# A hybrid encoder step on one core: attention's steps are taken up 0.8 later by the planner's clock

## The chip, the cores and the metric

One core of a Trainium2 chip runs the whole step as one program. The time is device microseconds of an execution; of the kernel before there are three, and the median counts. A further execution was profiled. The engines are TensorE (PE, with its weight loads as PEld), VectorE (DVE), ScalarE (ACT), GpSimd (POOL) and SyncE (SP), which starts most DMAs.

## The reference: what is computed

Two groups of rows (1024 of a prompt, 64 of a sample) go through one layer. Cut to what matters here:

```python
h = rms_norm(x, n_pre)
aq, af, ai, ag, bq, bk, bv, bg, cu, cg = split(h @ w_in)      # 1024 x 3584
# stick-breaking attention, 4 heads of 64, blocks of 128 queries
z = einsum('bqhd,bkhd->bhqk', q, k) * 64 ** -0.5
log_1m = where(mask, log_sigmoid(-z), 0)
after = cumsum(log_1m, reverse=True) - log_1m
w = where(mask, exp(log_sigmoid(z) + after), 0)
b_out = einsum('bhqk,bkhd->bqhd', w, v) * silu(bg)
x = x + rms_norm(concat([a_out, b_out, c_out]) @ w_out, n_post)
x = x + rms_norm(cross_attn(rms_norm(x, nx_pre), mem_k, mem_v), nx_post)
```

Beside attention stand an HGRN2 scan (a_out), a pooling mix (c_out) and the keys and values of 256 memory rows. All outputs are float32.

## The kernel before

**Tiling.** The 1088 rows are nine row tiles (i = 0 to 7 of 128 prompt rows, i = 8 of 64 sample rows), and three column chunks c = 0, 1, 2 of 384, 384 and 320 rows where activations lie transposed. Large products keep precision by splitting both operands into a high and a low half and adding three products (`mm3`, line 339): "main products" below are these, with tile name mm in the trace. `mm3` hands control back after every six products, so main work comes in groups of six; a projection of one chunk (`proj`, line 713) is 24 products, four groups.

**The order is planned.** The kernel is written as generators, and a planner (`Sched`, lines 43 to 100) decides in which order they are run on. Every helper (`mm`, `tr`, `act`, `tt` and so on) adds a cost for its instruction to a clock for its engine (`op`, line 56), and each task remembers when its last results on each engine are due (`dep`). A task's ready time is the latest of these due times, TensorE's left out, or the time at which what it waits for by name was done, plus the task's `slack` (`ready`, line 71). Main is the last task in the list. The planner runs the first task whose ready time has passed on its TensorE clock, so any other task that is ready goes ahead of main, and main's groups fill the time between. A task that gives control back is looked at again at the next such point. A product of 384 columns and high and low halves costs max(0.113, 384 / 2400 + 0.005) us by that clock (line 170).

The planner's order is the order in which instructions are written down, and with it their priority. The program builder then places them with a reckoning of its own: where a buffer is not free by that reckoning, a later instruction can go first. Instructions under `urgent()` (evacuations of main products, splits of weights) are given a higher priority.

**The stage around the change.** After the HGRN2 heads, main projects bq, bk and bv of head pair 0, then of pair 1 (`keys_values`, line 947); each chunk of bv spawns a small task, `bv{j}{c}`, that transposes the values to rows. While pair 1 is projected, w_out is loaded and split in three pieces (`load_wide`, line 1011; tiles wraw, hhi, hlo). Main then goes over the row tiles: `side` (line 1193) splits a row tile of the mixed heads (C), `wide` (line 1203) multiplies it by w_out in pieces of 384, 384 and 256 columns (four groups each), and `wide_norm` normalizes and adds the residual. Row tile i waits for `("sb", 0, i)` and `("sb", 1, i)`, which attention marks as done.

Attention is one task, `sb` (`sb_all`, line 614), spawned with the first chunk's values of pair 0. Its 26 units (13 to a pair) are a row tile's queries against up to 512 keys; row tiles 4 to 7 take two units. A step of the task is `scores` of unit k, `values` of unit k - 2 and `weights_T` of unit k - 1, then it gives control back:

- `scores` (line 629): three products and a mask for each of the two heads of the pair, on the upper and the lower 64 rows, into two banks of the PSUM tiles hg (three in all); for each head two sigmoids on ScalarE, a scan (line 650) and a product on VectorE, tile sm.
- `weights_T` (line 658): up to eight transposes (tp) and two copies on ScalarE (wT).
- `values` (line 677): up to sixteen products (hg from wT and vb); at a row tile's last unit VectorE multiplies the bank into C.

Pair 1's units wait for `bv10`, `bv11` and `bv12` where they begin to need them (line 703). When `sb` is finished, the next row tile to end closes attention's buffers and opens those of the next norm (`open_h2`, line 1172), whose task `h2` runs with a slack of 2.0.

Of the kernel before, what the change touches and what calls it, by code (L numbers as in the profile page):

```python
# [104 lines left out]
def hybrid_step(  # L105
# [38 lines left out]
    sch = Sched()  # L144
# [5 lines left out]
    def ps_tp():  # L150
        return ps.tile([P, 512], F32, tag="tp", name="tp", bufs=2)
# [21 lines left out]
    def tr(out, in_, n):  # L173
        sch.op("PE", 0.11)
        PE.transpose(out, in_, ident[:n, :n])  # L175

    def act(out, in_, func, **kw):
        t = TABLE.get(func)
        sw = 1.3 if t is not None and t != cur.get("table") else 0.0
        if t is not None:  # L180
            cur["table"] = t
        sch.op("ACT", 0.2 + sw + free(in_) / 1200.0)
        cur['ACT'] = ACT.activation(out, in_, func, **kw)  # L183
# [20 lines left out]
    def urgent():  # L204
        return tc.high_priority(offset=URGENT)
# [83 lines left out]
    def split(src, hi, lo):  # L289
        act(hi, src, AF.Copy)  # L290
        sub(lo, src, hi.bitcast(F32))
# [421 lines left out]
    def proj(wb, c, hT, every=6):  # L713
        t0, n = CHUNKS[c]
        o = ps_mm()
        hhi, hlo = hT[c]
        yield from mm3(o[:, :n], [(wb[0][:, k], wb[1][:, k], hhi[:, k, :n], hlo[:, k, :n]) for k in range(KT)], every)
        cur["o"] = o
# [14 lines left out]
    def main():  # L733
# [4 lines left out]
        pool = TP("start", "right")  # L738
# [9 lines left out]
        def prefetch(i):  # L748
            if i < len(names):
                kind, j = names[i]  # L750
                src = w_xk[j] if kind == "mk" else w_xv[j] if kind == "mv" else w_in[COL[kind] // P + j]
                if i < 2:
                    wq[i] = [wpool([P, KT, P], F32, "wraw", 2), wpool([P, KT, P], F32R, "whi", 2),
                             wpool([P, KT, P], F32R, "wlo", 2), {}]
                    first.append(wq[i])
                    for ks in (slice(0, 4), slice(4, 8)):
                        SP.dma_start(wq[i][0][:, ks], src[:, ks])
                else:
                    wq[i] = wblock(src)
# [184 lines left out]
        st, sbops = {}, {}  # L944
        wo, wdeps = [], []

        def keys_values(bi, j, wbs, q):


            kh = pool([P, KEYS], F32R, "kh", 2)  # L950
            kl = pool([P, KEYS], F32R, "kl", 2)
            ck = pool([P, P], F32, "ck", 1)
            SP.dma_start(ck, cache_sb_k[j * P:(j + 1) * P, :])
            split(ck, kh[:, SEQ:SEQ + P], kl[:, SEQ:SEQ + P])
            vb = pool([P, NT, P], F32, "vb", 2)
            cv = pool([P, P], F32, "cv", 2)
            SP.dma_start(cv, cache_sb_v[0, 0, :, 2 * j:2 * j + 2, :])
            sbops[j] = (q, (kh, kl), vb, cv)
            rows, cs = slice(j * P, (j + 1) * P), slice(j * P, (j + 1) * P)
            for c, (t0, n) in enumerate(CHUNKS):  # L960
                n1 = min(n, SEQ - t0)
                sch.fresh(**wbs[0][2])
                yield None
                yield from proj(wbs[0], c, hT)
                o = cur["o"]
                kr = pool([P, 384], F32, "kr", 3)
                with urgent():
                    split(o[:, :n1], kh[:, t0:t0 + n1], kl[:, t0:t0 + n1])
                    if n1 < n:
                        split(o[:, n1:n], kh[:, SEQ + P:], kl[:, SEQ + P:])  # L970
                    act(kr[:, :n], o[:, :n], AF.Copy)
                SP.dma_start(p_sb_k[rows, t0:t0 + n1], kr[:, :n1])
                if n1 < n:
                    SP.dma_start(s_sb_k[rows, :], kr[:, n1:n])
                sch.fresh(**wbs[1][2])
                yield None
                yield from proj(wbs[1], c, hT)
                o = cur["o"]
                vr = pool([P, 384], F32, "kr", 3)
                with urgent():  # L980
                    act(vr[:, :n], o[:, :n], AF.Copy)

                def values_tm(vr, c, t0, n, n1):
                    yield None
                    if c:
                        yield f"bv{j}{c - 1}"
                    pt = ps_tp().rearrange("p (c t) -> p c t", t=P)
                    i0, full = t0 // P, n1 // P
                    for i in range(full):
                        tr(pt[:, i, :], vr[:, i * P:(i + 1) * P], P)  # L990
                    if n1 < n:
                        tr(pt[:SMP, full, :], vr[:, n1:n], P)
                    act(vb[:, i0:i0 + full, :], pt[:, :full, :], AF.Copy)
                    SP.dma_start(p_sb_v[0, 0].rearrange("(i p) h d -> p i (h d)", p=P)[:, i0:i0 + full, cs],
                                 vb[:, i0:i0 + full, :])
                    if n1 < n:
                        act(vb[:SMP, 8, :], pt[:SMP, full, :], AF.Copy)
                        SP.dma_start(s_sb_v[0, 0].rearrange("p h d -> p (h d)")[:, cs], vb[0:SMP, 8, :])
                sch.spawn(values_tm(vr, c, t0, n, n1), f"bv{j}{c}")
                if (j, c) == (0, 0):  # L1000
                    sch.spawn(sb_all(sbops, pool), "sb")
                if j == 1:
                    b0, b1 = PIECES[c]
                    pair = [big([P, KT, n], F32R, f"{x}{c}") for x in ("hhi", "hlo")]
                    wdeps.append(load_wide(w_out, pair, range(b0, b1)))
                    wo.append((slice(b0 * P, b1 * P), *pair))
                elif c == 1:
                    prefetch(bi + 2)
                    prefetch(bi + 3)

        def load_wide(src, tiles, blocks):
            save, sch.cur = sch.cur, Sched.Task(None, "w")
            hi, lo = tiles
            for i, cb in enumerate(blocks):
                with urgent():
                    raw = wload(src[cb])
                    cs = slice(i * P, (i + 1) * P)
                    act(hi[:, :, cs], raw, AF.Copy)
                    sub(lo[:, :, cs], raw, hi[:, :, cs].bitcast(F32))
            dep, sch.cur = dict(sch.cur.dep), save  # L1020
            return dep
        for bi, (kind, j) in enumerate(names):
# [16 lines left out]
            if (kind, j) in (("bk", 0), ("bk", 1)):  # L1039
                wbs = [wq.pop(bi), wq.pop(bi + 1)]  # L1040
                yield from keys_values(bi, j, wbs, st["bq"])
# [17 lines left out]
            if kind in ("mk", "mv"):  # L1059
# [30 lines left out]
                if (kind, j) == ("mv", KT - 1):  # L1090
# [4 lines left out]
                    pool = TP("hgrn", "right")  # L1095
# [65 lines left out]
            elif kind == "bg" and j == 1:  # L1161
# [4 lines left out]
                pool = TP("sb", "right")  # L1166
# [293 lines left out]
```

## Time and profile before

| | us |
|---|---|
| three executions, median | 937.71 |
| lowest, highest | 934.66, 938.21 |
| profiled execution, its own time | 935.02 |
| its span | 933.3 |
| attention of pair 0, from its first scores | 441.6 to 494 |
| main products alone | 494 to 516.8 |
| attention of pair 1 | 516.8 to 576 |

The mean granted TensorE clock of the profiled execution is 0.996 of full speed. In the rows of the profile a line starts with the source line (L171 is the product helper, L175 the transpose, L183 ScalarE's, L187 VectorE's two-operand helper), then engine and operation, then output tile and input tiles with shapes, a count and times. In rows of a timeline the start comes first, then the length; a bracket at the end is the engine's idle time before it and what ended it. In rows of windows every engine has its busy time and, in brackets, its count of instructions, then come the granted clock, the DMA share and GB/s. Lengths of products include a modelled end and overlap, so that the starts tell the pace. PE's busy time counts overlaps once.

### The profile page before, as it was taken

What the parts mean: (1) busy time and instruction counts of PE and PEld (TensorE: products, weight loads), DVE (VectorE), ACT (ScalarE), POOL (GpSimd) and SP (SyncE); (2) the same over time, 40 slices, a digit from 0 to 9 for tenths busy, and PEclk for the clock granted to TensorE, in tenths of its full rate; (3) what the DMA queues carried; (4) which work ended last, traced back from release to release, by engine and by line L of the source; (5) the groups of instructions that cost most, each with busy time, mean ns of one, the idle gap of its engine ahead of it and who ended that gap; (6) DMA issues with size and microseconds to landing.
All of it is one profiled execution on the core that took longest, in us unless ns stands there. A gap on an engine that the chain in (4) does not pass through costs nothing.

```text
span 933.3 us, 18372 instructions
## 1 busy us (share of the span) xinstructions
PE 914.2 (98%) x7504; PEld 853.6 (91%) x7504; DVE 556.6 (60%) x1125; ACT 479.5 (51%) x1005; POOL 107.2 (11%) x194
## 2 busy tenths in 40 slices
PE   8899999999999999999999999999999999999997
PEld 7899999999998999989779788999999999999997
DVE  6849483674678574552684777565564545563343
ACT  7623384658767774963673765433452333342231
POOL 5502430010010010000000000211200000001110
PEclk9999999999999999999999999999999999999999
DMA  8815511011100111012111411222433111232231
GB/s 306 259 38 181 142 46 47 25 49 29 47 27 31 47 33 46 25 47 79 47 31 36 157 61 69 90 68 80 164 119 92 30 39 46 76 106 91 91 101 58
DMA packets 33126, 73.60 MB, mean 79 GB/s; under 512 B 5601, under 2 KB 18065, under 8 KB 33042
## 3 DMA queue, kind: packets, MB, share of 16 engines
q1 hardware_dynamic: 30112, 68.07, 22.7%
q0 software_dynamic: 1888, 4.35, 1.3%
q8 instruction: 59, 0.97, 0.4%
q14 instruction: 25, 0.20, 0.1%
q10 hardware_dynamic: 1042, 0.01, 0.1%
HBM read 56.45 MB, written 15.89 MB: 78 GB/s over the span
## 4 chain that ended last, share of the span: by engine, by line
PE 82%; DVE 6%; ACT 4%; DMA 4%; issue 2%; POOL 1%; DVEq 0%; POOLq 0%; ACTq 0%
PE mm L171 64%; PE hg L171 14%; PE tp L175 5%; DVE sm L650 3%; DVE sm L187 1%; DVE wlo L187 1%; ACT L183 1%; ACT whi L183 1%; DMA xt<-in_x_prompt_dram 1%; DVE hlo L187 1%; DMA wraw<-in_w_xk_dram 1%; DMA mkd<-mraw 1%; DMA wraw<-in_w_xo_dram 1%; DMA gT<-in_norm_mem_dram 1%; DMA mvd<-mtm 1%
## 5 line engine op out<-in xcount | busy, mean ns | idle before, releaser
L171 PE MATMUL mm<-hhi,whi 128*128 128x384 f32 (+2 forms) x1272 | 425.1, 334 | 0.0
L171 PE MATMUL mm<-hlo,whi 128*128 128x384 f32 (+2 forms) x1272 | 412.5, 325 | 0.0
L171 PE MATMUL mm<-hhi,wlo 128*128 128x384 f32 (+2 forms) x1248 | 405.3, 325 | 0.0
L171 PEld LDWEIGHTS mm<-hhi,whi 128*128 128x128 f32 x1272 | 239.2, 188 | 6.3 <-issue 1.3
L171 PEld LDWEIGHTS mm<-hlo,whi 128*128 128x128 f32 x1272 | 239.5, 188 | 1.2 <-issue 0.9
L171 PEld LDWEIGHTS mm<-hhi,wlo 128*128 128x128 f32 x1248 | 234.6, 188 | 0.4 <-issue 0.3
L187 DVE TENSOR_TENSOR wlo<-wraw,whi 128x1024 fp32r<-128x1024 f32 (+1 forms) x53 | 63.5, 1200 | 56.6 <-ACT whi L183 56.3
L183 ACT ACT_TABLE_LOAD x66 | 84.7, 1283 | 19.0 <-DVE E L187 12.0
L183 ACT ACTIVATE whi<-wraw 128x1024 fp32r<-128x1024 f32 (+1 forms) x53 | 55.3, 1043 | 71.5 <-PE mm L171 54.7
L183 ACT ACTIVATE wraw<-mm 128x384 f32<-128x384 f32 (+3 forms) x51 | 22.9, 449 | 72.8 <-PE mm L171 62.9
L650 DVE TENSOR_TENSOR_SCAN sm<-sm 128x384 f32<-128x384 f32 (+4 forms) x52 | 48.3, 938 | 14.0 <-ACT sm L183 14.0
L183 ACT ACTIVATE sm<-hg 128x384 f32<-128x384 f32 (+4 forms) x104 | 42.2, 485 | 15.7 <-PE hg L171 8.7
L187 DVE TENSOR_TENSOR wraw<-mm,gain 128x384 f32<-128x384 f32 (+1 forms) x48 | 24.4, 510 | 41.6 <-ACT wraw L183 41.3
L1241 POOL TENSOR_TENSOR small<-small 128x1 f32<-128x1 f32 (+1 forms) x18 | 4.2, 234 | 375.3 <-ACT wraw L183 375.3
L183 ACT ACTIVATE E<-E 128x512 f32<-128x512 f32 (+1 forms) x68 | 32.8, 515 | 10.5 <-DVE E L187 9.9
L171 PE MATMUL mm<-mhi,wlo 128*128 128x256 f32 x128 | 35.8, 289 | 1.8 <-DVE wlo L187 1.8
L321 POOL TENSOR_TENSOR small<-small,mhalf 128x1 f32<-128x1 f32 (+2 forms) x50 | 36.0, 719 | 4.2
L171 PE MATMUL mm<-mhi,whi 128*128 128x256 f32 x128 | 36.2, 293 | 0.1
L171 PE MATMUL mm<-mlo,whi 128*128 128x256 f32 x128 | 35.1, 283 | 0.0
L443 POOL COPY qf<-q 128x512 f32<-128x512 f32 (+1 forms) x12 | 14.6, 1218 | 177.6 <-PE hg L171 140.7
L187 DVE TENSOR_TENSOR wlo<-C,whi 128x1024 fp32r<-128x1024 f32 x16 | 19.6, 1225 | 24.9 <-ACT whi L183 23.4
L191 DVE SCALAR_TENSOR_TENSOR C<-wraw,small,C 128x384 f32<-128x384 f32 (+3 forms) x54 | 27.8, 569 | 10.2 <-POOL small L321 10.2
(209 smaller groups left out, 1409.1 us busy)
## 6 DMA issues: line engine op xcount, KB each, us to landing
wraw<-in_w_in_dram SPq DMA_DIRECT2D x28, 512.0 KB, 3.6
xt<-in_x_prompt_dram SPq DMA_DIRECT2D x8, 512.0 KB, 6.5
wraw<-in_w_xv_dram SPq DMA_DIRECT2D x8, 512.0 KB, 3.9
wraw<-in_w_out_dram SPq DMA_DIRECT2D x8, 512.0 KB, 3.6
C<-in_x_prompt_dram SPq DMA_DIRECT2D x8, 512.0 KB, 3.5
x1d<-C SPq DMA_DIRECT2D x8, 512.0 KB, 2.8
wraw<-in_w_xq_dram SPq DMA_DIRECT2D x8, 512.0 KB, 3.6
wraw<-in_w_xo_dram SPq DMA_DIRECT2D x8, 512.0 KB, 3.6
```

Of the source, the lines that this page charges most:

```text
L171: cur['PE'] = PE.matmul(out, lhsT=lhsT, rhs=rhs, start=start, stop=stop, skip_group_check=True)
L175: PE.transpose(out, in_, ident[:n, :n])
L183: cur['ACT'] = ACT.activation(out, in_, func, **kw)
L187: cur['DVE'] = DVE.tensor_tensor(out=out, in0=a, in1=b, op=op)
L191: DVE.scalar_tensor_tensor(out=out, in0=a, scalar=s, in1=b, op0=op0, op1=op1)
L321: POOL.tensor_tensor(out=r[:n, :w], in0=r[:n, :w], in1=mhalf[:n, :w], op=ALU.pow)
L443: POOL.tensor_copy(qf[:, 1, :], qq)
L650: DVE.tensor_tensor_scan(m[:nq, :n][:, ::-1], m[:nq, :n][:, ::-1], m[:nq, :n][:, ::-1], 1.0 if p is None else p[:nq, 0:1], ALU.mult, ALU.min)
L1241: POOL.tensor_tensor(out=ms[:n, 0:1], in0=ms[:n, 0:1], in1=ms[:n, pi:pi + 1], op=ALU.add)
```

## The change

The attention task is spawned with a slack of 0.8 where it had none. The slack is added to its ready time at every look that the planner takes at it, so it holds for each of its steps and for its waits by name.

```diff
@@ -998,7 +998,7 @@
                 sch.spawn(values_tm(vr, c, t0, n, n1), f"bv{j}{c}")
                 if (j, c) == (0, 0):
-                    sch.spawn(sb_all(sbops, pool), "sb")
+                    sch.spawn(sb_all(sbops, pool), "sb", 0.8)
                 if j == 1:
```

The code that reads it, unchanged:

```python
    def ready(self, t):
        if t.wait is not None:
            if t.wait not in self.done:
                return None
            return max([self.done[t.wait]] + [v for e, v in t.dep.items() if e != "PE"]) + t.slack
        return max([0.0] + [v for e, v in t.dep.items() if e != "PE"]) + t.slack
```

## The prediction

> **What bounds the kernel now.** I read the page's engine shares first, then the busy time of each engine by stage, then who makes TensorE wait in the attention's stage, and last the single steps in the timeline.
>
> ```profile
> span 933.3 us, 18372 instructions
> PE 914.2 (98%) x7504; PEld 853.6 (91%) x7504; DVE 556.6 (60%) x1125; ACT 479.5 (51%) x1005; POOL 107.2 (11%) x194
> ```
>
> TensorE is the bound. All its recorded idle time is 933.3 - 914.2 = 19.1 us, and only what lies where attention runs is within reach of an edit that respaces attention. Attention runs in two bursts, one for each pair of heads. The stages, with all engines (the columns after the length are busy time and count of PE, PEld, DVE, ACT, POOL):
>
> ```profile
> 441.50:494.00 52.50, 49.97 (x418) 40.01 (x418) 40.86 (x72) 36.27 (x89) 0.00 (x0) 1.00 0.13 39
> 494.00:516.80 22.80, 22.80 (x137) 22.53 (x135) 6.50 (x10) 8.43 (x14) 0.00 (x0) 1.00 0.26 84
> 516.80:576.10 59.30, 58.00 (x485) 45.22 (x484) 48.51 (x82) 42.26 (x105) 0.20 (x1) 1.00 0.21 68
> ```
>
> The same stretches, main products alone (tile mm):
>
> ```profile
> 441.50:494.00 52.50, 22.07 (x116) 18.50 (x116) 1.73 (x4) 3.41 (x8) 1.00 0.13 39
> 494.00:516.80 22.80, 22.72 (x132) 22.19 (x132) 2.16 (x4) 3.36 (x7) 1.00 0.26 84
> 516.80:576.10 59.30, 23.61 (x127) 19.44 (x126) 1.72 (x4) 3.15 (x9) 1.00 0.21 68
> ```
>
> Three things are in these rows. TensorE idles 52.50 - 49.97 = 2.53 us in the first burst and 59.30 - 58.00 = 1.30 us in the second, 3.83 us together. Between the bursts 132 main products, 22 groups of six, run with no attention beside them, in 22.72 us: 1.03 us a group. And the granted clock is 1.00 throughout, so no idle time is paid for twice. VectorE is busy for 78% and 82% of the two bursts: close enough to full that a single long instruction in its queue is felt. What TensorE waits for inside the bursts:
>
> ```profile
> PE tp L175 <- DVE sm L187: 2.3, 3, 1.3
> PE hg L171 <- DVE C L187: 0.9, 1, 0.9
> PE hg L171 <- ACT wT L183: 0.5, 2, 0.3
> ```
>
> That is 3.7 of the 3.83 us: the transposes wait for the weights from VectorE, value products wait for a PSUM bank that VectorE has not read out, and for weights that ScalarE has not copied. All of them are operands that are late at a step taken up too soon. The worst one, on PE and then on DVE:
>
> ```profile
> 458.52 0.31 PE L171 MATMUL mm<-hlo,whi 128*128 128x320 f32 x1
> 458.66 0.31 PE L171 MATMUL mm<-hhi,wlo 128*128 128x320 f32 x1
> 458.90 0.46 PE L171 MATMUL hg<-kh,qh 64*128 64x384 f32 x2
> ...
> 459.65 0.28 PE L171 MATMUL hg<-negmask,identb 128*128 128x128 bf16 x2
> 461.23 1.12 PE L175 MATMUL tp<-ident,sm 128*128 128x128 f32 x7 [1.30 <-DVE sm L187]
> ```
>
> ```profile
> 456.57 1.22 DVE L187 TENSOR_TENSOR wlo<-wraw,whi 128x1024 fp32r<-128x1024 f32 x1 [3.18 <-ACT whi L183]
> 457.71 0.42 DVE L187 TENSOR_TENSOR kl<-mm,kh 128x256 fp32r<-128x256 f32 x1
> 458.05 2.33 DVE L650 TENSOR_TENSOR_SCAN sm<-sm 128x512 f32<-128x512 f32 x2
> ...
> 460.41 1.28 DVE L187 TENSOR_TENSOR sm<-sm 128x511 f32<-128x511 f32 x2
> ```
>
> A weight's low half (1.22 us) and a key's (0.42 us) stand ahead of the scans, so the transposes start 1.30 us late.
>
> **The change, part by part.** Instructions are neither added nor removed; only the place of the attention's steps among the main products changes. The planner takes a step at the first boundary between groups of main products at which its TensorE clock has passed the step's ready time, so the overshoot now lies between nothing and one group. By the planner's own costs (line 170) a group of six is 6 x (384/2400 + 0.005) = 0.99 us, 0.83 us with 320 columns, 0.67 us with 256. With 0.8 added to the ready time, nearly every step goes one group later (with 384 columns when the overshoot is under 0.8 of 0.99; with 256 sometimes two). What an attention step issues is TensorE's products, ScalarE's sigmoids and copies and VectorE's scans and products; it starts no DMA, so no queue of SP or POOL is passed by it. The main products that come ahead of it bring their evacuations and the loads of w_out with them, and these start earlier against attention.
>
> Is there enough main work? The first burst has 13 steps before its units are scored, and needs 13 more groups; the 22 alone behind it give them, at no cost. In the second burst 127 products are 21 groups among 15 steps, and 9 of those groups now run alone, while attention waits for the last value block of its pair:
>
> ```profile
> 544.91 4.04 PE mm L171 x26
> ...
> 549.43 4.86 PE mm L171 x28
> ```
>
> With two groups to a step, main reaches that block after about five steps instead of eight, so this wait goes, and 30 groups in 15 steps reach some way into the second row tile of the output projection (9 groups of projections, then 12 to a row tile). Main does not run dry: its first row tile needs attention's first row tile of the second pair, which is read out two steps after it is scored, and comes up after nine groups, some four steps in. What is late next is the end of attention, by some 9 groups, 9 us, less what is saved. Behind it stands only the opening of the next norm's buffers, at the end of a row tile, so it may come one row tile (12 groups, 12.4 us) later. The cover for that:
>
> ```profile
> 588.69 1.05 ACT L183 ACTIVATE wraw<-C 128x1024 f32<-128x1024 f32 x1
> ```
>
> ```profile
> 600.00:610.00 10.00, 10.00 (x66) 9.97 (x64) 6.99 (x11) 4.11 (x11) 2.44 (x5) 1.00 0.31 107
> ```
>
> ```profile
> 667.96 13.53 PE mm L171 x78
> ```
>
> The norm's first tile starts at 588.69 and its first reader is the query projection at 667.96: 79 us for work that is caught up with VectorE at 70% and ScalarE at 41%, while TensorE stands at 10.00 of 10.00. I cost it at nothing; were the cover gone, the price would be one late tile, about the 1.3 us of such a stall.
>
> Now the gains. First, the idle 3.83 us. Second, waits that the modelled ends hide: sixteen value products take 1.58 us in the two short steps (64 queries) and 1.09 us elsewhere, so 0.49 us each, 0.98 us.
>
> ```profile
> 483.93 1.09 PE L171 MATMUL hg<-wT,vb 128*64 128x128 f32 x16
> 491.53 1.58 PE L171 MATMUL hg<-wT,vb 128*64 128x128 f32 x16 [0.27 <-ACT wT L183]
> 569.98 1.58 PE L171 MATMUL hg<-wT,vb 128*64 128x128 f32 x16 [0.26 <-ACT wT L183]
> ```
>
> Third, score pairs that have come apart. The two heads' scores run as pairs on the two halves of the rows; in three steps of the second burst the builder has placed one head at a time, because a bank is not yet free by its reckoning (ScalarE is splitting w_out there):
>
> ```profile
> 448.59 0.44 PE L171 MATMUL hg<-kh,qh 64*128 64x384 f32 x2
> 449.53 0.44 PE L171 MATMUL hg<-wT,vb 128*64 128x128 f32 x4
> 522.13 0.44 PE L171 MATMUL hg<-kh,qh 64*128 64x384 f32 x1
> 522.88 0.39 PE L171 MATMUL mm<-hhi,wlo 128*128 128x320 f32 x1
> 523.94 0.44 PE L171 MATMUL hg<-kh,qh 64*128 64x384 f32 x1
> 524.72 0.50 PE L175 MATMUL tp<-ident,kr 128*128 128x128 f32 x3
> 526.15 0.50 PE L171 MATMUL hg<-kh,qh 64*128 64x512 f32 x1
> 526.58 0.65 PE L175 MATMUL tp<-ident,sm 128*128 128x128 f32 x4
> 530.29 0.44 PE L171 MATMUL hg<-kh,qh 64*128 64x384 f32 x1
> 531.67 0.45 PE L171 MATMUL hg<-kh,qh 64*128 64x384 f32 x1
> ```
>
> A whole pair takes 449.53 - 448.59 = 0.94 us; apart, 0.75 + 0.78 = 1.53 us. The second visit also costs its two crossings: the start after 458.66 comes 0.24 us later instead of 0.14, so 0.1 on the way in and, as I estimate, as much out. A broken step costs 0.59 + 0.18 = 0.77 us; two are wholly broken and the one at 526.15 loses the 0.43 us of its lone product, 1.97 us in all. One more group gives ScalarE 1 us to free the banks.
>
> The sum: 3.83 + 0.98 + 1.97 = 6.8 us is what spacing could give. Of it stays: of the 1.30 us stall what a 320 column group (6 x 0.147 = 0.88 us) leaves, 0.4 us; another step that now meets a 1.22 us split, 0.3 us; one of the three broken steps, 0.7 us; and two extra visits where a new group parts steps that lie back to back, 0.4 us. 6.8 - 1.8 = 5.0 us. The profiled execution took 935.02 us (1.7 us beside its span), so 930.0 for one like it; it lies 2.7 us under the median of the runs shown, 937.71 (934.66 to 938.21), and on that median the forecast is 932.7 us. The bounds: all of it and more, or less than nothing if the steps come apart (below).
>
> The idle rows may not show all the room. In a step that nothing delays, the weight loads fill this much:
>
> ```profile
> 486.83:489.39 2.56, 2.56 (x28) 1.97 (x27) 2.46 (x4) 2.04 (x5) 0.00 (x0) 1.00 0.00 0
> ```
>
> 1.97 of 2.56 us is 77%. In the first burst 116 main products at 22.72 / 132 = 0.172 us take 20.0 us, all of it filled with loads, and attention's other 32.5 us at 77% would hold 25.0 us: 45.0 us of loads, where the row has 40.01. The second, 127 products or 21.8 us and 37.5 us at 77%, would hold 50.7, where the row has 45.22. That is 5.0 + 5.5 = 10.5 us short, at most, since some products are narrower than those of the 0.172 us; my sum above has 6.8. The Trainium skill, "Perfetto Trace Analysis", Identifying the Most-Contended Engine, says that matmul busy time misjudges TensorE's room because matmuls are pipelined, and that the loads' busy share is the better measure; by it the gain would be the larger one, and the trace of before cannot yet tell.
>
> **The rivals.** *More room than the idle rows show.* 10.5 - 1.8 = 8.7 us, 929.0 on the median. For it: the shortfall of loads just worked out. Against it: broken pairs and crossings lower the share of loads too, and are in my sum already.
>
> *The stalls only move.* The late operands come from 1.22 us splits that stand ahead in VectorE's queue; each still meets some step, and the builder places by its own reckoning, so that its order hardly follows the planner's. Then 0 to 2 us, 936 to 938. For it: VectorE's work is the same. Against it: with 13 more groups the first burst's VectorE share falls from 78% to 62%.
>
> *Slower: steps come apart.* The builder may fill the extra room by placing one head's scores at a time, as at 522 and 530. It decides from the point where the broken steps outweigh the rest of the gain: without the pairs that is 3.83 + 0.98 - 0.7 - 0.4 = 3.7 us, eaten by 5 steps of 0.77 us; 11 make the kernel slower by 4.7 us, and 12 of the 23 whole ones give 12 x 0.77 - 3.7 = +5.5 us, 943.2. For it: main's w_out splits now fall on fewer steps, and a crossing costs a tenth. Against it: the first burst has all 13 steps whole. The Trainium skill, "TensorEngine Tiling (Array Packing)", Key Properties, says that a change of tiling mode drains TensorE; the 0.24 against 0.14 us agrees, and by that rule every extra visit speaks against this edit.
>
> **How the numbers follow.** 0.5% of this kernel, 4.7 us, is about what a measurement of it can tell from no change. My forecast (2.5 to 7 us saved): 0.55, of which 0.30 over 4.7 us. More room: 0.12. Stalls move: 0.21. Steps come apart: 0.12. So faster by over 0.5%: 0.42; within: 0.25 + 0.21 = 0.46; slower: 0.12. The likeliest case's own range is 930.5 to 935. The range for 8 in 10 runs from 928.5 (the larger gain) to 939 (no gain, at the upper end of the runs), leaving out the broken steps and the far end of the gain.
>
> **What would show it.** Right: two groups, 12 main products, between most attention steps; the stretch without attention between the bursts falls from 22 groups to about 9, and that at 545 goes; PE idle in the bursts under 1.5 us; scores in pairs throughout; attention ends near 579. Wrong: one group as before (the edit did not reach the order); the idle rows still name DVE sm with over 2 us; more than 5 steps with single scores; or idle time after 580 that was not there.

## The result and the profile after

The changed kernel takes 929.28 us (median of five, 928.38 to 932.13), the kernel before 935.48 us (median of five, 934.02 to 938.21): a ratio of 0.994 with a 95% interval of 0.9923 to 0.9957, 6.2 us faster. Beside the last experiments it was timed again, 930.24 against 934.55 us, a ratio of 0.9955 (0.9939 to 0.997), 4.3 us. The forecast was 5.0 us less; as a time, 932.7 us, counted from the median of three, 937.71 us, that was known then.

The page of its profiled execution (930.88 us):

```profile
span 929.2 us, 18368 instructions
PE 911.1 (98%) x7504; PEld 853.1 (92%) x7504; DVE 556.8 (60%) x1125; ACT 479.6 (52%) x1005; POOL 107.7 (12%) x194
```

The number of instructions on each engine is as before. The bursts and what lies between them, all engines, then main products alone:

```profile
443.70:499.80 56.10, 55.02 (x454) 45.74 (x454) 42.69 (x72) 37.48 (x91) 0.00 (x0) 1.00 0.12 34
499.80:516.90 17.10, 17.10 (x100) 16.84 (x98) 6.22 (x10) 6.49 (x11) 0.00 (x0) 1.00 0.38 122
516.90:581.00 64.10, 63.01 (x533) 51.92 (x532) 51.48 (x88) 44.00 (x110) 1.86 (x4) 1.00 0.24 76
```

```profile
443.70:499.80 56.10, 27.84 (x152) 24.22 (x152) 2.68 (x6) 4.41 (x10) 1.00 0.12 34
499.80:516.90 17.10, 17.02 (x96) 16.49 (x95) 1.21 (x3) 2.46 (x5) 1.00 0.38 122
516.90:581.00 64.10, 31.36 (x175) 27.10 (x174) 3.17 (x7) 4.81 (x15) 1.00 0.24 76
```

Both bursts are longer and hold more main products, 152 for 116 and 175 for 127, and the stretch without attention is shorter, 96 products for 132. In the timeline 12 main products, two groups, lie between most steps where 6 or fewer lay before; the 54 products that ran alone near 545 are spread over the second burst.

The start of the kernel scatters from execution to execution (attention's first key transposes come at 441.25 us in this profile of the changed kernel and at 439.31 us in another), so I compare a stretch that holds the same work in every run: from the key transposes ahead of attention's first scores to the first product of row tile 8 (1605 products on TensorE). Before, and after:

```profile
440.11:660.44 220.33, 216.37 (x1606) 192.67 (x1605) 141.23 (x232) 119.11 (x283) 17.55 (x36) 1.00 0.21 71
```

```profile
441.25:656.39 215.14, 212.97 (x1605) 191.66 (x1604) 141.60 (x232) 119.00 (x283) 17.60 (x36) 1.00 0.22 73
```

The stretch is 5.2 us shorter; what follows it takes 272.8 and 272.9 us (929.2 - 656.4 and 933.3 - 660.4). Of the 5.2 us, idle time gives 3.96 - 2.17 = 1.8 us and TensorE's busy time 3.4 us. Busy time can shrink with the same products because it holds what the idle column doesn't show: waits inside merged rows, and pairs of scores that run one after the other. Both are gone in the short steps (1.09 us for 1.58) and at the three places where the pairs had come apart, two of which are shown:

```profile
497.69 1.09 PE L171 MATMUL hg<-wT,vb 128*64 128x128 f32 x16
...
524.81 0.45 PE L171 MATMUL hg<-kh,qh 64*128 64x384 f32 x2
...
529.67 0.51 PE L171 MATMUL hg<-kh,qh 64*128 64x512 f32 x2
...
573.04 1.09 PE L171 MATMUL hg<-wT,vb 128*64 128x128 f32 x16
```

What TensorE still waits for in the bursts:

```profile
PE tp L175 <- DVE sm L187: 1.1, 2, 0.8
PE hg L171 <- ACT sm L183: 1.1, 1, 1.1
```

Of the three kinds of late operands two are gone; the wait for weights from VectorE is halved, and one of 1.1 us is new: value products that wait for a bank which ScalarE's sigmoids have not yet read out.

```profile
466.54 1.09 PE L171 MATMUL hg<-wT,vb 128*64 128x128 f32 x16 [1.08 <-ACT sm L183]
```

### The profile page after: what moved, and what is told of

It reads as the page before. It is cut to its first block, busy times and chain, and to the rows that moved or that the text cites. A ratio compares the mean times of both kernels' runs of the same rounds, so it can differ in the third digit from the quotient of the medians.

```text
span 929.2 us, 18368 instructions
## 1 busy us (share of the span) xinstructions
PE 911.1 (98%) x7504; PEld 853.1 (92%) x7504; DVE 556.8 (60%) x1125; ACT 479.6 (52%) x1005; POOL 107.7 (12%) x194
## 4 chain that ended last, share of the span: by engine, by line
PE 87%; DVE 4%; ACT 3%; DMA 3%; issue 1%; POOL 1%; DVEq 0%; POOLq 0%; ACTq 0%
PE mm L171 66%; PE hg L171 16%; PE tp L175 5%; DVE sm L650 1%; ACT L183 1%; DVE hlo L187 1%; DVE wlo L187 1%; DMA wraw<-in_w_xk_dram 1%; DMA gT<-in_norm_mem_dram 1%; DMA xt<-in_x_prompt_dram 1%; DMA mkd<-mraw 1%; DMA wraw<-in_w_xv_dram 0%; ACT whi L183 0%; DMA wraw<-in_w_out_dram 0%; POOL small L321 0%
## 5 line engine op out<-in xcount | busy, mean ns | idle before, releaser
L183 ACT ACTIVATE E<-E 128x512 f32<-128x512 f32 (+1 forms) x68 | 32.8, 515 | 10.5 <-DVE E L187 9.8
L183 ACT ACTIVATE hhi<-tp 128x512 fp32r<-128x512 f32 (+1 forms) x36 | 19.1, 570 | 28.7 <-PE tp L175 28.6
```

## The experiments

Each was timed in turn with the kernel before on one chip. The stretch is the one of equal work, from the profiled execution; "busy" and "idle" are TensorE's in it, "rest" is what follows it, and "single" counts the rows in the bursts that show a first score product of one head alone.

| kernel | ratio to before (95%) | stretch | busy | idle | rest | single |
|---|---|---|---|---|---|---|
| before | 1 | 220.33 | 216.37 | 3.96 | 272.9 | 6 |
| the change, 0.8 | 0.994 (0.9923 to 0.9957) | 215.14 | 212.97 | 2.17 | 272.8 | 0 |
| 0.8, pair 0 only | 0.9974 (0.9961 to 0.9987) | 218.27 | 215.75 | 2.52 | 272.8 | 6 |
| 0.8, pair 1 only | 0.9967 (0.9951 to 0.9983) | 217.55 | 213.49 | 4.06 | 272.8 | 0 |
| 0.4 | 0.9959 (0.9942 to 0.9975) | 217.15 | 214.79 | 2.36 | 272.8 | 6 |
| 1.2 | 0.9975 (0.9962 to 0.9987) | 217.10 | 213.04 | 4.06 | 272.8 | 0 |
| 1.8 | 1.0036 (1.0024 to 1.0047) | 221.38 | 218.99 | 2.39 | 275.2 | 4 |
| 1.8 then 0.8 | 0.9957 (0.9944 to 0.9969) | 216.46 | 213.37 | 3.09 | 272.8 | 0 |
| 0.8 then 1.8 | 0.9978 (0.9966 to 0.999) | 215.09 | 212.60 | 2.49 | 275.3 | 0 |
| -0.8 | 1.0099 (1.0084 to 1.0115) | 229.51 | 223.77 | 5.74 | 272.8 | 16 |
| w_out's high halves on GpSimd | 1.0177 (1.0163 to 1.019) | 235.64 | 216.76 | 18.88 | 275.3 | 0 |
| w_in's low halves on GpSimd | 1.0009 (0.9995 to 1.0023) | 220.28 | 217.05 | 3.23 | 272.8 | 6 |
| the change again | 0.9955 (0.9939 to 0.997) | 215.41 | 212.84 | 2.57 | 272.8 | 0 |
| 0.8, heads one after the other | 0.9967 (0.9956 to 0.9978) | 216.74 | 213.67 | 3.07 | 272.7 | 4 |

### The two halves

The task changes its own slack where the second pair begins. For pair 0 only:

```diff
+            if k == nu // 2:
+                sch.cur.slack = 0.0
             if k < nu:
```

> The slack of 0.8 holds for the steps of head pair 0 only and is set to nothing at the first unit of pair 1. In the two profiles the stretch up to the second pair's values got shorter by 2.1 us, counted from the key transposes ahead of attention. Theory (each burst gains by its own late operands): the first burst's idle falls from 2.5 to about 1 us, and the kernel is 2 us faster than before, ratio 0.998. Rival (the gain is the second burst's whole score pairs alone, the first burst's difference is scatter): no change, ratio 1.000.

For pair 1 only, the task is spawned without a slack and sets 0.8 at the same place.

> No slack for head pair 0, 0.8 from the first unit of pair 1 on. Theory: the score pairs of the second burst stay whole, its short step no longer waits, and the stretch with main products alone near 545 goes; the kernel is 3 to 4 us faster than before, ratio 0.996 to 0.997, and with the run of the first pair alone the two gains add up to the whole 6 us. Rival (the gain is in the second burst alone): the whole 6 us, ratio 0.994. Rival (the first burst's spacing brings main forward and is needed for the second): under 1.5 us.

The two gains are 2.2 us (932.84 against 935.04) and 3.0 us (932.02), in the stretch 2.1 and 2.8 us; 4.8 us together, and the change itself has 5.2. So the halves add up, within what two stretches differ by, and no rival holds: the first burst's gain is no scatter, and the second does not need the first. The stretch of each, pair 0 only and pair 1 only:

```profile
440.52:658.79 218.27, 215.75 (x1605) 192.75 (x1604) 141.60 (x232) 119.24 (x283) 17.56 (x36) 1.00 0.22 72
```

```profile
444.58:662.13 217.55, 213.49 (x1605) 191.42 (x1604) 141.26 (x232) 118.86 (x283) 17.57 (x36) 1.00 0.22 72
```

The first burst's gain is mostly idle time (3.96 to 2.52 us), the second's is all busy time (216.37 to 213.49 us) at the idle time of before: in its rows no pair is parted, which by the prediction's prices is worth 1.97 us of these 2.9, and the short step of pair 1 another 0.49.

### How much slack

Only the number changes, to 0.4, to 1.2 and to 1.8.

> Slack 0.4. A step is moved by one group where the planner's overshoot is under 0.4, which with groups of 0.67 to 0.99 is 40 to 60% of the steps. Theory (each step moved gives its share): 2.5 to 3.5 us faster than before, ratio about 0.997. Rival (few steps hold all of the gain, and it is chance whether they move): anything between none and 6 us, and the idle rows show which steps were hit.

> Slack 1.2 for all steps, between the change and 1.8, which loses by a fall of the granted clock and by 2.5 us behind the stage. Theory (late operands go step by step with the spacing, and attention still ends in time for the next norm): as fast as with 0.8 or up to 1 us faster, ratio 0.992 to 0.995. Rival (the later end of attention already moves the norm's tiles against the weight loads, as in the run with 0.8 and 1.8, where that cost 2.5 us): 0.995 to 0.998.

> Slack 1.8: two groups more to a step than before, one more than with 0.8. Theory (late operands): the 2.2 us of idle that 0.8 leaves in the two bursts fall to 1 us or less, 1 us faster than with 0.8, ratio 0.992 to 0.994 of before. The first burst then needs 26 groups of the 22 that lay behind it, so it reaches up to the second pair. Rival (0.8 has taken what spacing can give; the later end of attention moves the next norm back): the same as with 0.8 or slower, 0.994 to 0.997.

0.4 gives 2.8 us (932.24 against 935.04), as the theory had it, with the pairs still parted. 1.2 gives 2.1 us (932.41 against 934.55), outside what the theory allowed, though attention's later end costs nothing there (rest 272.8 us), so the rival's reason is not it either: the idle time is back at 4.06 us. Its waits in the bursts are those of the kernel before in kind, at other steps, and the new one for a bank that ScalarE holds:

```profile
PE hg L171 <- ACT sm L183: 1.6, 1, 1.6
PE hg L171 <- DVE C L187: 1.3, 2, 0.9
PE tp L175 <- DVE sm L187: 0.8, 1, 0.8
PE hg L171 <- ACT wT L183: 0.3, 1, 0.3
```

So the recorded waits do not shrink step by step with the spacing; which step meets which queue seems to decide, and that 0.8 falls well is luck as far as these runs show. 1.8 is slower than before by 3.9 us, and both expectations missed why. Two stretches of its profile:

```profile
526.00:530.70 4.70, 3.42 (x23) 2.06 (x22) 3.24 (x4) 4.48 (x10) 0.00 (x0) 0.98 0.00 0
530.70:544.30 13.60, 13.60 (x48) 9.83 (x48) 10.98 (x16) 7.04 (x14) 0.00 (x0) 0.50 0.18 52
```

The third column from the end is the granted clock: half of full speed for 13.6 us, so up to 6.8 us lost, after 4.7 us with 23 products and 1.28 us of idle time. The mean clock is 0.989 to 0.993 in all twelve executions of this kernel and not under 0.995 in those of before, so it belongs to the kernel. The Trainium skill, "TensorE: Matmul & The Clock Gate", Part 1: The HAM clock gate, has the clock at half rate after an idle window of about 3.4 us; half rate agrees with the 0.50, but no idle gap of that length is there: the longest is 1.27 us. Nor does a gap of this size always do it: the kernel before waits 1.30 us ahead of 461.23, and its clock stays at 1.00.

> Slack 1.8 for head pair 0 and 0.8 for pair 1. With 1.8 for both, the granted clock was 0.50 from 530.7 to 544 us, some 13 us at half speed, 6 to 7 us lost, and that is all of its loss: without it the stage would be 0.6 us shorter than with 0.8. Theory (the clock falls because the first burst runs up to the second, so that steps with few main products follow each other from 511 to 531): the clock falls here too, and the kernel is as slow as with 1.8 for both, ratio 1.002 to 1.004. Rival (the second burst's first steps with 1.8 make it): the clock stays at 1.00 and the kernel is as fast as with 0.8 or 1 us faster, ratio 0.992 to 0.994.

> Slack 0.8 for head pair 0 and 1.8 for pair 1, the other half. Theory (the first burst's late end makes the clock fall): the clock stays at 1.00, ratio 0.992 to 0.995. Rival (the second burst's spacing makes it): the clock falls near 530, ratio 1.002 to 1.004. A third way: neither half alone does it, and both of these runs are at 0.992 to 0.995.

Neither half alone makes the clock fall (mean 0.996 or more in every execution of both). That is the third way of the expectation as to the clock, though both ratios, 0.9957 and 0.9978, lie above its range. What exactly tips it stays open; no run put filler products there. 1.8 then 0.8 gains 4.0 us (930.76 against 934.75), with an idle time of 3.09 us in a stretch 1.3 us longer than the change's. And 0.8 then 1.8 shows something else: its stretch is as short as the change's, and the rest is 2.5 us longer. Its norm's first tile comes at 604.98, the change's at 584.58 and that of before at 588.69. What TensorE then waits for, from 650 to 720 (in the change itself, 0.8 us for another operand and nothing else), and the chain there:

```profile
PE mm L171 <- DVE wlo L187: 1.1, 2, 0.6
PE mm L171 <- ACT whi L183: 0.5, 1, 0.5
PE tp L175 <- DVE wraw L191: 0.2, 1, 0.2
```

```profile
657.33 4.54 DMA wraw<-in_w_xq_dram
661.89 1.07 ACT whi L183
662.98 1.24 DVE wlo L187
664.24 3.64 DMA wraw<-in_w_xq_dram
```

The loads of w_xq have come onto the chain. They use the same two wraw buffers as the norm's tiles, which are now caught up in that time; that these buffers hold the loads back is how I read it, and no run gave them a third.

### Less room

The slack becomes -0.8.

> Slack -0.8: a step is taken up one group sooner than before where there is one to spare. Theory (too few main products between steps make the operands late): the waits in the two bursts grow from 3.8 us to 6 us or more, more pairs are parted, and the kernel is 3 to 8 us slower than before, ratio 1.003 to 1.009. Rival (spacing itself matters little, and the gain of 0.8 is where its steps happen to fall): within 2 us of before.

9.5 us slower (944.02 against 934.55), a little more than the theory allowed, though the waits in the bursts grew to 5.2 us and not to 6. Of the 9.2 us in the stretch, 1.8 are idle time and 7.4 busy time: 16 single rows for 6, and TensorE goes over from main products to attention only 15 times for 30 (key transposes not counted), so that steps lie back to back and wait inside their rows. The rival, within 2 us of before, fails. Up to 1.7 us of the busy time is something else that the expectation did not have: the clock fell here too, for 3.4 us, behind a stretch of 23 products with 1.21 us of idle time.

```profile
443.38:672.89 229.51, 223.77 (x1605) 198.00 (x1604) 142.56 (x232) 119.59 (x283) 16.92 (x36) 0.99 0.21 68
526.00:529.30 3.30, 2.09 (x23) 1.49 (x22) 2.32 (x9) 2.12 (x10) 0.00 (x0) 0.99 0.56 181
529.30:532.70 3.40, 3.40 (x19) 2.45 (x16) 2.86 (x7) 2.19 (x6) 0.00 (x0) 0.50 0.00 0
```

### What makes the operands late

On the kernel before, without a slack, work is taken out of a queue. First w_out's high halves, from ScalarE to GpSimd:

```diff
-                    act(hi[:, :, cs], raw, AF.Copy)
+                    if src is w_out:
+                        sch.op("POOL", 2.0)
+                        POOL.tensor_copy(hi[:, :, cs], raw)
+                    else:
+                        act(hi[:, :, cs], raw, AF.Copy)
```

> The kernel before, no slack; the high halves of w_out are copied by GpSimd and not by ScalarE, eight instructions of 1.05 us off ScalarE's queue, most of them in the second burst. Theory (ScalarE's splits keep the banks, so that the builder parts the score pairs): the pairs near 522 to 532 stay whole and the second burst is 1.5 to 2 us shorter, ratio 0.998, if GpSimd's copies are done in time. Rival (VectorE or the order of the steps parts them): the pairs stay parted, ratio 1.000. A wait of main for w_out would show as idle time of the products mm and make it slower.

Then the low halves of the last three blocks of w_in, from VectorE to GpSimd:

```diff
-            split(raw, hi, lo)
+            if lo_pool:
+                act(hi, raw, AF.Copy)
+                sch.op("POOL", 2.0)
+                POOL.tensor_tensor(out=lo, in0=raw, in1=hi.bitcast(F32), op=ALU.subtract)
+            else:
+                split(raw, hi, lo)
```

> The kernel before, no slack; the low halves of the three last blocks of w_in are computed by GpSimd and not by VectorE, so two of 1.22 us leave VectorE's queue inside the first burst. Theory (these stand ahead of the scans and make the transposes late): the first burst's idle falls from 2.5 us by 1 to 2 us and the stretch by as much, ratio 0.998 to 0.999. Rival (VectorE is simply full, and the wait moves to another step): the same idle, ratio 1.000.

With ScalarE freed of w_out the pairs stay whole (no single rows), as the theory has it. The planner's costs moved with the work, though, and with them the order of the steps, so this agrees with the theory and does not prove it. Its time says nothing of what whole pairs are worth: the kernel is 17 us slower, the order of the second burst and of the norm has changed, the granted clock is 0.50 for 3.4 us behind a wait of 1.57 us, and TensorE waits for VectorE's norm rows and weights:

```profile
PE tp L175 <- DVE wraw L191: 10.0, 7, 1.5
PE tp L175 <- DVE sm L187: 5.8, 4, 1.7
```

With VectorE freed of w_in's low halves the time is that of before, as the rival has it: 0.7 us of idle time have become 0.7 us of busy time. The long wait of 1.30 us is gone, but there are five shorter ones for the weights where there were three:

```profile
PE tp L175 <- DVE sm L187: 2.5, 5, 0.9
PE hg L171 <- ACT wT L183: 0.5, 2, 0.3
```

### What a parted pair costs

The changed kernel, with the loops over the heads and the three products exchanged:

```diff
-            for pi, (q, k) in enumerate(((qh, kh), (qh, kl), (ql, kh))):
-                for e in range(2):
+            for e in range(2):
+                for pi, (q, k) in enumerate(((qh, kh), (qh, kl), (ql, kh))):
```

> The changed kernel (slack 0.8), but every unit's scores are written out for one head after the other instead of in turn, so that all 26 pairs are parted, each without a second visit. Theory (a parted pair costs what the rows near 522 show: 0.59 us at 384 keys, in proportion to the keys 9600 / 384 x 0.59 = 14.8 us over all units): 14 to 15 us over the changed kernel, ratio to the kernel before 1.008 to 1.011. Rival (the two heads' products do not run side by side, and the visits were the cost): as fast as the changed kernel, ratio 0.994.

It is 1.25 us slower than the change beside it by the medians (931.49 against 930.24), with executions that overlap, and 1.3 us by the stretch. So the theory, 14 to 15 us, fails. The rival's time is nearly met, but not its reason, as the rows show. This kernel at one of the two places where key transposes came between the heads, and at a unit of 512 keys:

```profile
450.87 0.46 PE L171 MATMUL hg<-kh,qh 64*128 64x384 f32 x1
451.16 0.34 PE L171 MATMUL hg<-kl,qh 64*128 64x384 f32 x1
451.44 0.55 PE L175 MATMUL tp<-ident,kr 128*128 128x128 f32 x3
451.91 0.44 PE L171 MATMUL hg<-kh,ql 64*128 64x384 f32 x1
451.92 0.44 PE L171 MATMUL hg<-kh,qh 64*128 64x384 f32 x1
...
478.00 0.51 PE L171 MATMUL hg<-kh,qh 64*128 64x512 f32 x2
478.33 0.41 PE L171 MATMUL hg<-kl,qh 64*128 64x512 f32 x2
478.57 0.41 PE L171 MATMUL hg<-kh,ql 64*128 64x512 f32 x2
478.92 0.28 PE L171 MATMUL hg<-negmask,identb 128*128 128x128 bf16 x2
```

The first products of both heads start together although three of the first head stand ahead of the second's, in the source and in the built program: 0.92 us from the first score to the mask, as in the change itself (478.41 to 479.32, 0.91 us). Two heads that follow each other directly run side by side in either order. What costs is other work on all rows between the two, as the kernel before had near 522. The changed kernel has key transposes at the same two places, but behind the first products of both heads, and there its rows take 1.40 us to the mask for 1.77 (and 1.35 for 1.56 at the other place):

```profile
451.66 0.44 PE L171 MATMUL hg<-kh,qh 64*128 64x384 f32 x2
452.04 0.55 PE L175 MATMUL tp<-ident,kr 128*128 128x128 f32 x3
452.51 0.44 PE L171 MATMUL hg<-kl,qh 64*128 64x384 f32 x2
452.79 0.33 PE L171 MATMUL hg<-kh,ql 64*128 64x384 f32 x2
453.06 0.28 PE L171 MATMUL hg<-negmask,identb 128*128 128x128 bf16 x2
```

These two places are 0.6 us of the 1.3; another 0.5 us is idle time (3.07 for 2.57). So a step's score pairs are cheap to keep: their products need only be neighbours.

### The change again

The changed kernel without any edit, on the chip that ran -0.8, 1.2 and the exchanged loops.

> The changed kernel itself beside the other runs of this call, so that they can be compared on one chip: ratio 0.992 to 0.996 of before.

930.24 against 934.55 us, with a stretch of 215.41 us for 215.14 in the first profile. The 0.3 us between the two profiles of one kernel is all there is to judge a difference of stretches by; the 1.3 us to the exchanged loops and the 1.7 us to 1.2 are larger, but each rests on one profile.

## Why the prediction was right

**The sum** was 5.0 us; the stretch of equal work shows 5.2, the medians 6.2 and 4.3. The mechanism is there in the rows, step by step, but that the sum came out so closely is luck: its two terms were mis-sized against each other, the idle time by 1.3 us too much and the busy time by 1.6 us too little. As a time, 929.28 us lies below the 930.5 to 935 us of the likeliest case and near the 929.0 us of the larger gain. That is mostly the start of the count, since the kernel before came out at 935.48 us for 937.71; the gain itself, 6.2 or 4.3 us, lies within the 2.5 to 7 us forecast.

**The idle time** was to give 3.83 - 0.4 - 0.3 = 3.1 us. It gave 1.8, and the sign "idle in the bursts under 1.5 us" was missed with 2.17: the wait for the weights fell from 2.3 to 1.1 us and not to some 0.7, and 1.1 us for a bank held by ScalarE came new, which I had not looked for. The reason I gave for the lateness, single 1.22 us splits ahead in VectorE's queue, holds for the worst wait alone: with these splits moved off VectorE's queue the waits for weights were 2.5 us against 2.3, in five pieces instead of three, so one wait gives way to others. That was the argument of the rival "the stalls only move", and the run with 1.2 shows it at work; its time, no gain, did not come. What I held against it was wrong in size: VectorE's share of the first burst fell from 78% to 76% (42.69 of 56.10 us), not to 62%, since the burst grew by 3.6 us and not by 13 groups.

**The busy time** was to give 0.98 + 1.97 - 0.7 - 0.4 = 1.85 us. It gave 3.4: none of the three pairs stayed parted, both short steps went from 1.58 to 1.09 us, and no visits to attention were added (29 for 30). The rows account for 1.97 and 0.98 us of the 3.4 at the prediction's prices. In two other pairs key transposes stand between the products, so that "pairs throughout" is not quite what came. That ScalarE's splits of w_out part the pairs agrees with the run that moved them, and is not shown beyond that.

**Where the steps go**: one group more at nearly every step, as worked out from the planner's costs, and the stretch near 545 went. The first burst took fewer groups than I counted, and 96 products are left alone behind it, 16 groups and not 9: of its twelve gaps nine grew by a group, two stayed at 6 products, and one of 30 shrank to 12, while the second burst begins a group later. The last value products start at 580.76 for 575.87 before; I had said near 579.

**The cover** behind attention held: the norm's first tile came earlier, at 584.58, and idle time there did not grow. That it is not endless the run with 0.8 and 1.8 shows, where the price is 2.5 us and not the 1.3 I had named.

**More room than the idle rows show** was right in kind and not in size: 3.4 of 5.2 us came out of busy time. The weight loads' unfilled time in the stretch fell from 27.7 to 23.5 us, 4.2 us, of the 10.5 us that I had worked out by the loads. The Trainium skill, "Perfetto Trace Analysis", Identifying the Most-Contended Engine, is borne out that far: the matmul's busy time hid the larger part of what there was to win.

**Steps that come apart** did not come with 0.8 or 1.2, but with less room: -0.8 has eight, and is the slow case that this rival described. With 1.8 there are two.

## What to carry to other kernels

Where a planner interleaves steps that wait for each other with work that does not, look at its overshoot: if a step is taken up the moment its operands are expected, a margin of one block of filler is worth trying; here it cost nothing behind the stage as long as the next stage still began in time. Try it in sizes, since its effect is not even: here 0.8 beat 0.4 and 1.2 by 1.7 to 2.0 us in the stretch, and 1.8 lost. Measure it on a stretch of equal work, as idle time showed less than half of the gain here, and look at the granted clock as well.

## What the runs showed of the hardware

TensorE's granted clock fell to 0.50 for 13.6 us in a burst whose longest idle gap was 1.27 us, and the loss (up to 6.8 us) was larger than the 5.2 us that spacing won here; it fell for 3.4 us behind gaps of 1.21 us (-0.8) and 1.57 us (w_out's high halves on GpSimd), and stayed at 1.00 behind one of 1.30 us in the kernel before. Products on the upper and lower 64 rows run side by side when they are neighbours, whether they are issued in turns or head by head: 0.91 and 0.92 us for six of 512 columns. A 128x1024 difference took 2.49 us on GpSimd and 1.22 us on VectorE, and GpSimd's copy of that size with rounding 1.15 us, ScalarE's 1.05 us.
